# A mixture of experts as one large product: the first two stages of product 1 split a third time, their weight sums made in the first phase

## The chip, the cores and the metric

The kernel runs on one core of one Trainium2 chip. The metric is the device time of one execution in microseconds; for the kernel before it is the median of three runs, 1366.98 us (1366.88 to 1367.12). One more execution was taken by the hardware profiler: 1367.07 us, with a span from the first to the last instruction of 1365.1 us.

## The reference

16 x 512 = 8192 tokens with 512 values each, 8 experts, and a weight matrix of 512 x 2048 for each expert. Every token goes through all experts; the results are weighted by the softmax of its router logits and added up:

```python
probs = softmax(router_logits)                      # (16, 512, 8)
for e in range(8):
    output += probs[:, :, e:e+1] * np.matmul(x, expert_weights[e])
```

Since the weight of an expert can be multiplied into x first, this is one matrix product: 8192 rows, an inner dimension of 8 x 512 = 4096 (expert and hidden value), and 2048 columns.

## The kernel before

**Levels.** The kernel computes this product with the Strassen scheme (Winograd's form), in which a product of 2 x 2 blocks takes seven block products and some sums. On the outer level, the tokens come in pairs of blocks of 256 rows (`NHQ` = 32 blocks, 16 pairs, counted by `q`), the inner dimension in experts 0 to 3 and 4 to 7, the columns in two halves of 1024. The seven outer products are called 1 to 7; product 1 is the even block, experts 0 to 3, and the first column half. `product(r, q)` makes outer product `r` of pair `q`.

On the second level each outer product is split once more: 128 rows, two experts (eight chunks of 128, `K8`), 512 columns. Its seven **steps** go in the order 1, 5, 6, 2, 7, 3, 4 (`STEPS`, line 344). A step is eight TensorE matmuls of 128 x 128 by 128 x 512 into one PSUM bank (`Product.step`, line 543); `post` (line 551) then moves the bank on: a copy by ScalarE, or an addition by VectorE.

On the third level, which only some stages use, steps 1 and 5 of two products that run side by side are split again (`Split`, line 595, and `Third`, line 623). For each of the two steps there are seven **parts** of four matmuls of 128 x 128 by 128 x 256, named x1 to x7 for step 1 and q1 to q7 for step 5. The left side needs four sums of the two products' operands (tile `s`, `Third.make`), the right side four sums of blocks of the weight (tile `t`, `Split.make`), one set for each of the weights 1 and 5. Parts 6 and 7 are each followed by an addition on VectorE within PSUM (line 666), part 5 by two copies on ScalarE (lines 661 to 663).

**Left operands.** x times the probability, `z`, is made by VectorE from a transposed block `xT` and probabilities `pT` spread over all partitions (`times`, line 432). A stage's operands are `z` for the first two experts, the difference `d` of its token halves (`queue_s2`), `z` for the other two experts, and a combined one (`queue_i`).

**Weights.** Weight sums 5, 6, 7 and 4 of product 1 (tile `w`) are differences of the blocks in `b11` (`inner_sums`, line 169). Each takes one VectorE instruction of 4096 columns.

**The first phase** (lines 308 to 340) has no Strassen in it. It computes outer product 1 of pairs 0 and 1: four token tiles of 128 rows (`j`), two column halves (`n`), four experts (`e`), four chunks (`c`), 128 matmuls in all. Its left side `z0` is made by TensorE, which multiplies x by a diagonal matrix of probabilities (`early_z0`, line 246). In its second half (`n` = 1) TensorE also transposes blocks 4 to 7 for stage 0 (`early_xp1`, line 260; the casts out of PSUM are made by VectorE for `xT` and by ScalarE for `pT`), and VectorE makes weight sum 5. Its results go out through ScalarE copies and SyncE stores (lines 335 to 338). The softmax of all tokens is made meanwhile (`softmax_of_all`, line 284) and stored, so that later stages can load their probabilities.

**Stages.** After it come the stages, lists of one or two products that run step by step in turn (`run`, line 875). Stages 0 to 5 are product 1 of pairs 2 to 13, two pairs each. Stages 2 to 5 are split a third time (line 1219); the eight `t` sums for product 1 are queued in stage 1 (line 1221). When the next stage is split, the last two steps of a stage are held back (`held`, line 896) and run between the parts of the next: one behind parts 1 and 5, one behind parts 2 and 6 (`run_third`, line 856).

**What sets the order.** In the first phase a scheduler may move an instruction ahead on its engine, except on VectorE and ScalarE (`dve` and `act`, line 105), which keep the order of the program text. From line 342 on every engine keeps it. There the order of VectorE's work comes from a planner: work is put into `queue` with a cost, `slack` (line 375) takes from it while the planner's clock for VectorE is behind that for TensorE, and `need` (line 365) takes everything up to a task that must be there now. `at(stage, slot, ...)` hangs work on a place in a stage. Before stage 0, lines 1234 to 1242 fill the queue by hand: `z` of both products, weight sum 6, both `d`, the other `z`, weight sums 7 and 4.

**Buffers.** Weight tiles, `s` and `t` share one pool of 15 buffers (`wpool`, line 64); PSUM tiles come from a pool of 8 (line 95).

Of the kernel before, what the change touches and what calls it, by code (L numbers as in the profile page):

```python
# [31 lines left out]
def kernel(  # L32
# [7 lines left out]
    nc = tc.nc  # L40
    P = 128
    f16 = mybir.dt.float16
# [34 lines left out]
    def half():  # L77
        return h_tile([P, NB], f32)
# [43 lines left out]
    def sp(o, i):  # L122
        note(nc.sync.dma_start(out=o, in_=i))
# [7 lines left out]
    def mm(ps, z, w, start, stop):  # L131
        note(nc.tensor.matmul(ps, z, w, start=start, stop=stop, skip_group_check=True))  # L132
# [3 lines left out]
    def new_w():  # L136
        return wpool.tile([P, K8, NB], f16, name="w", tag="w")
# [122 lines left out]
    def early_xp1(j, d):  # L260
# [6 lines left out]
        mm(ps, ones, d.rearrange("p e t -> p (e t)"), True, True)  # L267
        evacuate(xp1[t][1][:, :, rows], ps.rearrange("p (e t) -> p e t", e=HE), 1)

    R = 4  # L270
    J = HQ // R
    p_dram = dram.tile([NHQ, 3 * HE, HQ], f16, name="p_dram")
# [32 lines left out]
                for c in (2 * g, 2 * g + 1) for j in (2 * h, 2 * h + 1)]  # L305
    ORDERS = [(c, j) for c in range(C) for j in range(4)], QUARTERS

    ds_ = [diag_e(0)]
    early_z0(0, ds_[0], (0, 1))
    for i in range(3):  # L310
# [4 lines left out]
    for e in (1, 2):  # L315
        ds_.append(diag_e(e + 1))
        early_z0(e, ds_[e])
    for n in range(2):
        ps = [bank() for _ in range(4)]
        for e in range(HE):  # L320
            if n == 0 and e == 1:
                early_z0(3, ds_[3])
                ph0.append(early_p(1))
                ds_ = [diag_j(j) for j in range(4, 8)]
                keep_p = softmax_of_all()
                w, sums = inner_sums(b11, new_w())
            for c, j in ORDERS[n == 0 and e == 0]:
                mm(ps[j], z0[j][:, e, c], b11[e // 2, n][:, e % 2 * C + c, :],
                   e + c == 0, e == HE - 1 and c == C - 1)
            if n == 1:  # L330
                for j in ((4, 5), (6, 7), (), ())[e]:
                    early_xp1(j, ds_[j - 4])
                if e == 1:
                    sums[5]()
        for j in range(4):
            o = half()
            act(nc.scalar.copy(o, ps[j]))
            sp(kept[j // 2][n].rearrange("(p j) m -> j p m", j=2)[j % 2], o)
        if n == 0:
            keep_p()  # L340

    ordered[0] = True
# [247 lines left out]


    THIRD = (1, 5)
    COLS = [ds(i * HQ, HQ) for i in range(2)]

    class Split:

# [8 lines left out]

        def make(self, p, i):
            if i == 0:
                self.t[p] = wpool.tile([P, 4, C, HQ], f16, name="t", tag="w")
            w, t = self.right.op(p), self.t[p]
            block = lambda k, n: w[:, ds(k * C, C), COLS[n]]  # L610
            x, y = ((block(0, 1), block(0, 0)), (block(1, 1), t[:, 0]), (block(1, 1), block(0, 1)),
                    (block(1, 0), t[:, 1]))[i]
            tt(t[:, i], x, y, SUB)

        def op(self, p, m):
            if m in (1, 2, 3):
                k, n = ((0, 0), (1, 0), (1, 1))[m - 1]
                return self.right.op(p)[:, ds(k * C, C), COLS[n]]
            i = {5: 0, 6: 1, 7: 2, 4: 3}[m]
            need(self.task[p, i])  # L620
            return self.t[p][:, i]

    class Third:
# [592 lines left out]
            post(p)  # L1216
    finish.step, finish.post = step_at_end, post_at_end

    for stage in (2, 3, 4, 5):
        third(stage, 1)  # L1220
    at(1, 2, splits[1].queue)
    for stage in (9, ):
        third(stage, 2)
    at(8, 2, splits[2].queue)
# [6 lines left out]
        third(stage, 3)  # L1231
    at(k3, 9, splits[3].queue)

    need_first = [right[1].task[p] for p in (6, 7, 4)]
    for p in (2, 3):
        lefts[1, p].queue_make(0)
    queue.append(need_first[0])
    for p in (2, 3):
        lefts[1, p].queue_s2()
    for p in (2, 3):  # L1240
        lefts[1, p].queue_make(1)
    queue.extend(need_first[1:])
    start_loads(1)
    store_loads(0)
    finish_loads(1)
# [30 lines left out]
```

## Time and profile before

| | before |
|---|---|
| median of 3 runs | 1366.98 us |
| profiled execution | 1367.07 us |
| its span | 1365.1 us |
| TensorE (PE) busy | 1359.9 us |
| VectorE (DVE) busy | 1126.5 us |
| ScalarE (ACT) busy | 195.7 us |
| matmuls | 6657 |
| VectorE instructions | 1367 |

In the profile PE is TensorE's matmuls, PEld its weight loads, DVE VectorE, ACT ScalarE, POOL GpSimd, SP SyncE, which only issues transfers. A row of the order of time shows the start in us from the first instruction, the duration in us, engine, line, operation, what is written and read with its shape, and xN for N like instructions in a row; behind it stands in brackets how long the engine had been idle and what released it. A row of the chain shows start, duration and what the end of the span hung on. A row of the waits shows the total, the number and the longest, in us. A row of busy time by stretches shows the stretch, its length, then the busy us of PE, PEld, DVE, ACT and POOL with the number of instructions, the granted clock, the busy share of the DMA engines and GB/s. All helpers issue through a few lines, so nearly all of VectorE's work has line 112 and TensorE's line 132; instructions are told apart by their tiles.

### The profile page before, as it was taken

The page shows a single profiled execution, that of the slowest core. Times are in us where ns is not written, and L with a number is a line of the kernel's source. Part 1 is how long each engine was busy: PE and PEld are TensorE (multiplying, and loading weights), DVE is VectorE, ACT ScalarE, POOL GpSimd, SP SyncE. Part 2 cuts the span into 40 slices and gives each one's busy share as a digit, 9 for nine tenths or more (in the row PEclk, how much of TensorE's full clock was granted, in tenths as well). Part 3 has the DMA queues.
Part 4 walks back from the last instruction along what each step waited for, and adds up shares of the span by engine and source line. Part 5 has one row for each costly group of instructions (what it writes and reads, how often), then busy time and mean ns, then how long its engine had stood idle before and what let it go on. Part 6 is the DMA issues. An engine that isn't in the chain of part 4 may idle for free.

```text
span 1365.1 us, 18194 instructions
## 1 busy us (share of the span) xinstructions
PE 1359.9 (100%) x6657; PEld 648.7 (48%) x6657; DVE 1126.5 (83%) x1367; ACT 195.7 (14%) x362; POOL 407.0 (30%) x644
## 2 busy tenths in 40 slices
PE   9999999999999999999999999999999999999998
PEld 4455544544444444444444444444444444456554
DVE  5975787989789788788887888888889797998873
ACT  3232311100011111111111100000000000123221
POOL 3123333331223342333322122242332422223232
PEclk9999999999999999999999999999999999999999
DMA  9999999999898999999999978989898979999896
GB/s 195 242 218 228 253 242 323 310 300 383 257 304 268 311 350 274 293 279 292 328 258 331 344 247 221 216 240 203 232 252 220 252 203 292 302 217 245 196 206 119
DMA packets 193385, 356.41 MB, mean 261 GB/s; under 512 B 53136, under 2 KB 87184, under 8 KB 188176
## 3 DMA queue, kind: packets, MB, share of 16 engines
q0 software_dynamic: 88048, 183.02, 55.3%
q1 hardware_dynamic: 99488, 132.25, 31.9%
q10 hardware_dynamic: 5760, 39.99, 7.6%
q8 instruction: 52, 0.85, 0.2%
q14 instruction: 37, 0.30, 0.1%
HBM read 214.47 MB, written 167.97 MB: 280 GB/s over the span
## 4 chain that ended last, share of the span: by engine, by line
PE 99%; DMA 0%; DVE 0%; issue 0%; ACT 0%; POOLq 0%
PE ps L132 99%; DMA w<-in_x_dram 0%; DVE z L238 0%; DVE h L112 0%; ACT h L1213 0%; POOLq L1260 0%
## 5 line engine op out<-in xcount | busy, mean ns | idle before, releaser
L132 PE MATMUL ps<-w,z 128*128 128x512 f16 x5240 | 1125.7, 375 | 0.0
L132 PEld LDWEIGHTS <-z 128*128 128x128 f16 x5328 | 521.2, 98 | 598.4
L126 POOL DMA_DIRECT2D out_dram<-h x380 | 249.3, 662 | 736.5 <-ACT h L582 352.6
L112 DVE TENSOR_TENSOR h<-ps,h 128x512 f32<-128x512 f32 x415 | 284.6, 687 | 184.7 <-PE ps L132 166.7
L112 DVE TENSOR_TENSOR z<-xT,pT 128x2048 f16<-128x2048 f16 x216 | 261.9, 1217 | 0.0
L132 PE MATMUL ps<-w,d 128*128 128x512 f16 x880 | 199.1, 379 | 0.0
L132 PEld LDWEIGHTS <-d 128*128 128x128 f16 x880 | 86.1, 98 | 101.5
L112 DVE TENSOR_TENSOR z<-z,d 128x2048 f16<-128x2048 f16 x110 | 131.7, 1217 | 0.0
L582 ACT COPY h<-ps 128x512 f32<-128x512 f32 x64 | 37.5, 585 | 524.5 <-PE ps L132 521.1
L112 DVE TENSOR_TENSOR w<-w 128x1024 f16<-128x1024 f16 (+2 forms) x88 | 100.0, 1146 | 1.8 <-PE ps L132 1.0
L571 ACT COPY h<-ps 128x512 f32<-128x512 f32 x90 | 52.7, 585 | 293.5 <-PE ps L132 264.1
L112 DVE TENSOR_TENSOR ps<-ps,h 128x512 f32<-128x512 f32 (+1 forms) x110 | 64.0, 585 | 26.0 <-PE ps L132 25.7
L112 DVE TENSOR_TENSOR d<-z 128x1024 f16<-128x1024 f16 x110 | 74.6, 687 | 5.1 <-PE ps L132 3.6
L568 ACT COPY h<-ps 128x512 f32<-128x512 f32 x90 | 51.8, 589 | 132.4 <-PE ps L132 129.6
L126 POOL DMA_DIRECT2D kept<-h x56 | 30.8, 549 | 110.9 <-ACT h L571 78.0
L126 POOL DMA_DIRECT2D wd<-w x78 | 44.2, 592 | 35.0 <-DVE w L112 27.5
L126 POOL DMA_DIRECT2D w<-in_expert_weights_dram x65 | 48.6, 778 | 19.5 <-issue 13.8
L112 DVE TENSOR_TENSOR u<-xT,pT 128x2048 f16<-128x2048 f16 x38 | 46.2, 1217 | 0.0
L112 DVE TENSOR_TENSOR h<-h 128x512 f32<-128x512 f32 (+2 forms) x69 | 45.1, 675 | 0.1
L112 DVE TENSOR_TENSOR z<-z,u 128x2048 f16<-128x2048 f16 x34 | 41.3, 1216 | 0.1
L112 DVE TENSOR_TENSOR z<-z 128x2048 f16<-128x2048 f16 x32 | 39.1, 1222 | 0.7
L564 ACT COPY ps<-ps 128x512 f32<-128x512 f32 x45 | 25.6, 570 | 94.4 <-PE ps L132 87.2
(61 smaller groups left out, 291.9 us busy)
## 6 DMA issues: line engine op xcount, KB each, us to landing
out_dram<-h POOLq DMA_DIRECT2D x380, 256.0 KB, 6.8
pT<-p_dram SPq DMA_DIRECT2D x125, 256.0 KB, 6.3
h<-kept SPq DMA_DIRECT2D x116, 256.0 KB, 6.7
w<-wd ACTq DMA_DIRECT2D x25, 1024.0 KB, 9.0
xT<-x SPq DMA_DIRECT2D x76, 256.0 KB, 6.8
w<-in_expert_weights_dram POOLq DMA_DIRECT2D x35, 512.0 KB, 10.9
wd<-w POOLq DMA_DIRECT2D x64, 256.0 KB, 6.6
h<-out_dram SPq DMA_DIRECT2D x60, 256.0 KB, 5.4
```

Of the source, the lines that this page charges most:

```text
L112: dve(nc.vector.tensor_tensor(out=o, in0=a, in1=b, op=op))
L126: note(nc.gpsimd.dma_start(out=o, in_=i, **how))
L132: note(nc.tensor.matmul(ps, z, w, start=start, stop=stop, skip_group_check=True))
L564: act(nc.scalar.copy(self.banks["b"], x))
L568: act(nc.scalar.copy(o[tn], q if p == 5 else x))
L571: act(nc.scalar.copy(o[TN[p]], b if p == 2 else x))
L582: act(nc.scalar.copy(o[tn], b))
```

## The change

The third level is used in stages 0 and 1 too, and with that several things move:

- The four `t` sums of weight 1 are made in the first phase: one ahead of the first products, three behind the last `z0`, ahead of the second softmax. The four of weight 5 are made behind weight sum 5, which itself comes one expert earlier. The `t` sums in stage 1 are gone.
- The last eight matmuls of the first phase (`n` = 1, `e` = 3, `c` = 2 and 3) are no longer made there. They are held as two lots of four and run in stage 0's places for held steps; the ScalarE copies and SyncE stores of these results follow the second lot.
- Stages 0 and 1 each get their left sums `s`, the parts, the additions and the copies. Before stage 0 the queue is filled with `z` of both products, the `s` sums, and weight sum 6, and emptied up to this; then come both `d`, the other `z`, and weight sum 7. Weight sum 4 is queued at the start of stage 0.
- In stage 0, the loads for stage 1 are issued ahead of the stores of the first phase's results, since these come later in the program.

In the order of the changed program VectorE has, from the casts of blocks 4 and 5: `xT` (2 casts), weight sum 5, four `t`, `xT` of blocks 6 and 7 (2 casts), two `z`, four `s`, weight sum 6, then stage 0's additions. TensorE has the transposes of blocks 4 to 7 five products into `n` = 1, `e` = 1, with some of that expert's products among them. From stage 2 on the order of every engine is as before, but for the eight `t`.

```diff
+    def third_weights(w, t, i):
+        block = lambda k, n: w[:, ds(k * C, C), COLS[n]]
+        x, y = ((block(0, 1), block(0, 0)), (block(1, 1), t[:, 0]), (block(1, 1), block(0, 1)),
+                (block(1, 0), t[:, 1]))[i]
+        tt(t[:, i], x, y, SUB)
...
+    early_t = {}
+
+    def early_thirds(p, some=range(4)):
+        if p not in early_t:
+            early_t[p] = new_t()
+        for i in some:
+            third_weights(w[p], early_t[p], i)
...
+    w, sums = inner_sums(b11, new_w())
+    early_thirds(1, (0,))
     for n in range(2):
         ps = [bank() for _ in range(4)]
         for e in range(HE):
             if n == 0 and e == 1:
                 early_z0(3, ds_[3])
+                early_thirds(1, (1, 2, 3))
                 ph0.append(early_p(1))
...
-                w, sums = inner_sums(b11, new_w())
             for c, j in ORDERS[n == 0 and e == 0]:
-                mm(ps[j], z0[j][:, e, c], b11[e // 2, n][:, e % 2 * C + c, :],
-                   e + c == 0, e == HE - 1 and c == C - 1)
+                if n == 0 or e < HE - 1 or c < 2:
+                    first_product(ps, n, e, c, j)
             if n == 1:
                 for j in ((4, 5), (6, 7), (), ())[e]:
                     early_xp1(j, ds_[j - 4])
-                if e == 1:
+                if e == 0:
                     sums[5]()
-        for j in range(4):
-            o = half()
-            act(nc.scalar.copy(o, ps[j]))
-            sp(kept[j // 2][n].rearrange("(p j) m -> j p m", j=2)[j % 2], o)
+                    early_thirds(5)
         if n == 0:
+            first_results(ps, n)
             keep_p()
...
-    for stage in (2, 3, 4, 5):
+    for stage in (0,1,2,3,4,5):
         third(stage, 1)
-    at(1, 2, splits[1].queue)
+    splits[1].t = early_t
...
+    def last_first(c):
+        for j in range(4):
+            first_product(ps, 1, HE - 1, c, j)
+        if c == C - 1:
+            first_results(ps, 1)
+
+    for c in (2, 3):
+        held.append(lambda c=c: last_first(c))
     need_first = [right[1].task[p] for p in (6, 7, 4)]
     for p in (2, 3):
         lefts[1, p].queue_make(0)
+    thirds[0].queue_sums()
     queue.append(need_first[0])
+    flush(need_first[0])
+    clock["dve"] = 0.0
     for p in (2, 3):
         lefts[1, p].queue_s2()
     for p in (2, 3):
         lefts[1, p].queue_make(1)
-    queue.extend(need_first[1:])
+    queue.append(need_first[1])
+    at(0, 0, lambda: queue.append(need_first[2]))
     start_loads(1)
```

`first_product` and `first_results` are the matmul and the copy with its store of before, made into functions; `new_t` makes a `t` tile. `Split.make` now calls `third_weights`, and `Split.op` asks for a queued task only where there is one.

More of the change, by code (lines that the diff above doesn't have):

```diff
@@ L268, in early_xp1, with new_t @@
         evacuate(xp1[t][1][:, :, rows], ps.rearrange("p (e t) -> p e t", e=HE), 1)
+    COLS = [ds(i * HQ, HQ) for i in range(2)]
+    def third_weights(w, t, i):
[3 more added lines that the diff above has]
+        tt(t[:, i], x, y, SUB)
+    def new_t():
+        return wpool.tile([P, 4, C, HQ], f16, name="t", tag="w")
+    early_t = {}
[4 more added lines that the diff above has]
+            third_weights(w[p], early_t[p], i)
     R = 4
@@ L306, with first_product, first_results @@
     ORDERS = [(c, j) for c in range(C) for j in range(4)], QUARTERS
+    def first_product(ps, n, e, c, j):
+        mm(ps[j], z0[j][:, e, c], b11[e // 2, n][:, e % 2 * C + c, :],
+           e + c == 0, e == HE - 1 and c == C - 1)
+    def first_results(ps, n):
+        for j in range(4):
+            o = half()
+            act(nc.scalar.copy(o, ps[j]))
+            sp(kept[j // 2][n].rearrange("(p j) m -> j p m", j=2)[j % 2], o)
     ds_ = [diag_e(0)]
@@ L592 @@
     THIRD = (1, 5)
-    COLS = [ds(i * HQ, HQ) for i in range(2)]
     class Split:
@@ L607, in make @@
             if i == 0:
[L608 to L613, printed above, removed]
+                self.t[p] = new_t()
+            third_weights(self.right.op(p), self.t[p], i)
         def op(self, p, m):
@@ L619, in op @@
             i = {5: 0, 6: 1, 7: 2, 4: 3}[m]
-            need(self.task[p, i])
+            need(self.task.get((p, i)))
             return self.t[p][:, i]
@@ L1232 @@
     at(k3, 9, splits[3].queue)
+    def last_first(c):
+        for j in range(4):
+            first_product(ps, 1, HE - 1, c, j)
[3 more added lines that the diff above has]
+        held.append(lambda c=c: last_first(c))
     need_first = [right[1].task[p] for p in (6, 7, 4)]
```

## The prediction

> **What bounds the kernel now.** I read the page first (busy shares and the chain that ended last), then the chain in order of time, then who waited on TensorE.
>
> ```profile
> span 1365.1 us, 18194 instructions
> PE 1359.9 (100%) x6657; PEld 648.7 (48%) x6657; DVE 1126.5 (83%) x1367; ACT 195.7 (14%) x362; POOL 407.0 (30%) x644
> ...
> PE 99%; DMA 0%; DVE 0%; issue 0%; ACT 0%; POOLq 0%
> ```
> ```profile
> 8.62 0.63 DVE h L112
> 9.25 0.05 issue
> 9.30 1352.25 PE ps L132 x6612
> ```
> ```profile
> PE every L94 <- DVE zero L91: 1.3, 1, 1.3
> PE ps L132 <- DVE h L112: 0.3, 1, 0.3
> ```
>
> From 9.30 us to the last product the chain is one unbroken piece of TensorE work, and TensorE's only waits on another engine lie before that. So time changes in two ways only: by the number and width of the products after 9.30 us, and by a stop of TensorE that isn't there now. What VectorE saves or spends counts only where TensorE comes to wait for it. The prices of products are read off the order of time on TensorE, first the start and stage 0, then a stage that is split a third time already:
>
> ```profile
> 1.30 4.45 PE L94 MATMUL every<-zero 128*128 128x512 f16 x10 [1.30 <-DVE zero L91]
> ...
> 7.50 1.50 PE L132 MATMUL ps<-h,w 128*128 128x128 f16 x24
> 9.30 1.07 PE L132 MATMUL ps<-h,w 128*128 128x128 f16 x16 [0.29 <-DVE h L112]
> ...
> 14.55 13.98 PE L132 MATMUL ps<-w,z 128*128 128x512 f16 x64
> 28.36 0.39 PE L132 MATMUL ps<-ident,w 128*128 128x128 f16 x4
> 28.58 0.38 PE L132 MATMUL ps<-h,ones 128*128 128x512 f16 x1
> ...
> 33.57 13.98 PE L132 MATMUL ps<-w,z 128*128 128x512 f16 x64
> ```
> ```profile
> 109.19 0.60 PE L132 MATMUL ps<-t,s 128*128 128x256 f16 x4
> 109.62 0.60 PE L132 MATMUL ps<-w,z 128*128 128x256 f16 x4
> 110.06 0.60 PE L132 MATMUL ps<-t,s 128*128 128x256 f16 x4
> 110.50 2.76 PE L132 MATMUL ps<-w,z 128*128 128x512 f16 x16
> ```
>
> A product 512 wide costs (28.36 - 14.55) / 64 = 0.2158 us from start to start. Groups of four 256 wide start 0.437 us apart, so one costs 0.109 us. The durations in the rows are longer, because products overlap.
>
> **What the split takes away.** In an unsplit stage, steps 1 and 5 of two products are 4 x 8 = 32 products 512 wide: 6.91 us. Split, they are 14 parts of 4, 56 products 256 wide: 6.11 us. Each stage saves 0.79 us, two stages **1.59 us**. Nothing else of TensorE's work changes in amount: the eight last products of the first phase move into stage 0, four behind the first parts and four behind the next, and the transposes of blocks 4 to 7 (28.36 us) fall among the first phase's second half.
>
> **The weight sums (t).** The eight sums leave stage 1, where VectorE has them at 76 to 81 us, and go into the first phase. Here are VectorE's rows of before, first its phase and stage 0, then the sums and the additions of a split stage:
>
> ```profile
> 14.08 1.29 DVE L238 CAST z<-ps 128x512 f16<-128x512 f32 x2 [1.84 <-PE ps L132]
> ...
> 22.86 2.20 DVE L112 TENSOR_TENSOR h<-h 128x512 f32<-128x512 f32 x4
> 28.78 1.29 DVE L238 CAST xT<-ps 128x512 f16<-128x512 f32 x2 [3.72 <-PE ps L132]
> 33.12 1.29 DVE L238 CAST xT<-ps 128x512 f16<-128x512 f32 x2 [3.04 <-PE ps L132]
> 34.44 2.29 DVE L112 TENSOR_TENSOR w<-w 128x4096 f16<-128x4096 f16 x1
> 36.65 2.35 DVE L112 TENSOR_TENSOR z<-xT,pT 128x2048 f16<-128x2048 f16 x2
> 38.92 2.28 DVE L112 TENSOR_TENSOR w<-w 128x4096 f16<-128x4096 f16 x1
> ...
> 59.76 0.69 DVE L112 TENSOR_TENSOR h<-ps,h 128x512 f32<-128x512 f32 x1
> ...
> 67.35 0.69 DVE L112 TENSOR_TENSOR s<-z 128x1024 f16<-128x1024 f16 x1
> ```
> ```profile
> 76.36 0.69 DVE L112 TENSOR_TENSOR t<-w 128x1024 f16<-128x1024 f16 x1
> ...
> 78.90 0.69 DVE L112 TENSOR_TENSOR t<-w 128x1024 f16<-128x1024 f16 x1
> ...
> 81.43 1.45 DVE L112 TENSOR_TENSOR h<-ps,h 128x512 f32<-128x512 f32 x2
> ...
> 90.42 0.87 DVE L112 TENSOR_TENSOR ps<-ps,h 128x256 f32<-128x256 f32 x2 [1.82 <-PE ps L132]
> ```
>
> Four t cost 81.43 - 78.90 = 2.53 us. The first four (of weight 1) are free: one fits into the 1.84 us of idle ahead of the last z0 casts at 14.08, the other three push the softmax chain from an end at 25.06 us to about 26.9, inside the 3.72 us of idle ahead of 28.78. If that cover were gone, the same 1.9 us would fall on the xT casts, and on the chain below. The second four (of weight 5) have no such cover: in the changed program they stand between sum 5 and the xT casts of blocks 6 and 7, and the first left operands (z) wait behind these.
>
> **Stage 0: who is late.** TensorE still begins its e=2 products at 33.57 us, but now only 24 of them come before stage 0: it gets there at 33.57 + 24 x 0.2158 = 38.75. Part x1 takes 0.44, and at **39.19** it wants part x5, whose left operand is the first sum of the two z (s). VectorE's path to it, with the rows' durations and their usual overlap of 0.08 us (none between an instruction and one that needs its result): the transposes of block 5 now start at 30.31 (28.36, and ahead of them seven first-phase products, block 4's four transposes, 0.22, and the product with ones, 0.22), their cast ends 30.31 + 0.39 + 0.03 + 0.69 = 31.42; sum 5 to 33.63; four t to the next start at 36.19; two xT casts to 37.40; two z, 37.40 to 39.75; s from 39.78 to 40.47. With 0.05 us to TensorE (VectorE ends at 9.25, TensorE resumes at 9.30) x5 starts at 40.52: a **stop of 1.33 us**. Before, stage 0 had no s and began at 33.57 + 32 x 0.2158 = 40.48, with its z ready at 37.9.
>
> Further on in stage 0 nothing more waits, but narrowly. Behind s stand its three others (to 42.52) and sum 6 (to 44.73), then the two additions of parts 6, to 45.08 and 45.52. Parts x7 and q7, which add into the columns that these read, come at 45.30 and 45.74, by the count below. I take nothing for it, and 0.3 us as the upper end.
>
> **Stage 1: the same once more.** From 40.52: x5, q1, q5 (1.31), four products (0.86), four parts (1.75), four products (0.86), six parts (2.62) end at 47.93; eight unsplit steps of 8 x 0.2158 = 1.73 end at 61.74; then stage 1's x1, and at **62.18** its x5. VectorE has by then, in the changed order, step 7's second result (its products end at 58.29, VectorE 58.49 to 59.18), z of one product (to 60.32), the first result of step 3 (60.24 to 60.93), z of the other (to 62.07), then the second result of step 3 (to 62.68), and only then s (62.60 to 63.29). x5 starts at 63.34: a **stop of 1.16 us**. What is queued behind here is s behind a result that TensorE itself finishes at 61.74; it is not a matter of lacking work time, so a quicker VectorE ahead of it would win little.
>
> The loads that stage 1 needs don't decide. SyncE's rows:
>
> ```profile
> 42.61 1.12 SPq L123 DMA_DIRECT2D pT<-p_dram  x2
> ...
> 44.80 6.22 SPq L407 DMA_TRANSPOSE xT<-w  x4
> ```
>
> In the changed order these stand ahead of the last stores of the first phase, no longer behind them, and even at the old times z at 59.1 has 8 us to spare. In later split stages VectorE has room:
>
> ```profile
> 84.00:107.50 23.50, 23.50 (x139) 13.37 (x137) 15.30 (x21) 6.94 (x14) 7.34 (x12) 1.00 0.98 234
> ```
>
> 15.3 us of 23.5 is VectorE's share in a split stage. So stage 2, which loses the t ahead of it, isn't late, and what is queued from there on stands as before. Stages 0 and 1 gain eight s (0.63 each) and eight additions (0.43): 8.5 us of VectorE work, none of which counts but for the two stops. ScalarE gains eight copies and is idle most of the time.
>
> **Sum.** -1.59 + 1.33 + 1.16 = +0.90 us on the profiled execution's 1367.07 us: 1367.97. The median of the runs is 0.09 lower, 1366.98, so I forecast **1367.9 us**. A stop's restart isn't in the trace at this length; I take 0.05 us, the one at 9.30, with 0 and 0.2 as ends. That and the narrow places give the forecast a range of its own of 1367.3 to 1368.6.
>
> **A rule that speaks against the saving.** The rows put a 256 wide product at 0.109 / 0.2158 = 0.51 of a 512 wide one; the split pays as long as that is under 32 / 56 = 0.57. The Trainium skill, page "TensorE: Matmul & The Clock Gate", section "Back-to-back issue gap", says that in streams of weight load and product the spacing is set by both, 81 ns at 128 columns and 131 ns at 512. An estimate midway from that page, some 98 ns at 256, would make the ratio 0.75 and the two stages 2.6 us longer where I count 1.59 shorter. The trace disagrees, with 0.2158 us at 512, and 0.109 at 256 in the very pattern that is added.
>
> **The rivals.**
> - *Both operands come in time, or one does.* VectorE is idle 17% of the span and 3.0 us just ahead of the row at 33.12. But the first sum stands behind everything counted above in program order, and moving 1.3 us out of that order needs an error in several rows. One stop alone gives 1366.7, none 1365.4; that is also the fastest that the change can be. Chance 0.10.
> - *More short stops*, at x7 and q7 of stage 0 (margins 0.2 us), with the same again in stage 1: 1368.6 to 1369.4. Chance 0.04.
> - *The clock falls when TensorE stops* (slower). The first ten products, 512 wide, took 4.45 / 10 = 0.44 us each, twice the later price; by the row at 7.50 the 128 wide ones run at 1.50 / 24 = 0.06. So the array was at half speed from 1.30 us to 7.50 at the latest, and such a stretch costs up to half its 6.2 us, 3.1 us. The stop of 0.29 us at 9.30 didn't bring it back; no stop of 1.3 us is in the trace. If the point lies between, one fall gives up to 1371.0 and two give up to 1374.1. For it: the same idle engine was slow at the start. Against: the granted clock is shown at 1.00 all along and these stops are a fraction of the stretch that it took to warm. Chance 0.07. The same page, section "What's actually happening", has half rate come back after an idle window of about 3.4 us; by that rule stops of 1.3 us leave the time at my forecast.
> - *Narrow products cost more than the trace shows*, by the rule above: the saving turns round and the stops remain, 1366.98 + 2.6 + 2.5 = 1372.1. Chance 0.01.
>
> **How the numbers follow.** The forecast has 0.78. The range, 1366.8 to 1369.2, takes in its own range and the nearer parts of the first two rivals; the clock, the case without a stop and the last rival stay outside, under 0.2 together. 0.2% is 2.73 us, about what a measurement of this kernel can tell from no change. Faster by that (under 1364.25) needs more than the whole saving: 0.01. Slower by that (over 1369.7) is the clock or the narrow products: 0.08. Within: 0.91.
>
> **What would show it.** Right: 48 more products in the changed profile; groups of four 256 wide 0.437 us apart in stages 0 and 1; TensorE waiting for VectorE's s twice, near 39 to 40.5 and 62 to 63.3 us, 1.1 to 1.4 us each; none later; 512 wide products at 0.216 us after each. Wrong: no wait for s (first rival), products at 0.4 us after a stop (clock), a wait at parts x7 and q7, or a wait for a load in stages 1 to 3.

## The result and the profile after

The kernel after takes **1374.4 us**, median of four runs (1372.3 to 1375.02); the kernel before took 1367.05 us beside it (1366.88 to 1367.13). The ratio is 1.005 with a 95% interval of 1.0038 to 1.0062: the change makes the kernel half a per cent slower. The profiled execution took 1375.02 us, 7.95 more than that of before. The page of after, in the same parts as before's (span, busy shares, the shares of the chain that ended last):

```profile
span 1373.1 us, 18308 instructions
PE 1361.0 (99%) x6705; PEld 652.8 (48%) x6705; DVE 1134.5 (83%) x1383; ACT 198.2 (14%) x370; POOL 407.0 (30%) x644
...
PE 88%; DMA 6%; issue 4%; POOL 1%; DVE 1%; SPq 0%; POOLq 0%; ACT 0%; DVEq 0%
```

The 48 products more that were counted are there (6705 against 6657), and so are the 16 VectorE instructions. But TensorE's share of the chain fell from 99% to 88%, and transfers hold 6% of it. The waits of TensorE, as total, number and longest, say where:

```profile
PE ps L132 <- DVE h L112: 3.6, 2, 3.3
PE ps L132 <- DVE s L112: 2.2, 2, 1.2
```

Two waits for `s` were forecast. The wait of 3.3 us for an `h` was not. TensorE's order of time at the first two, and then at the third:

```profile
10.59 3.63 PE L132 MATMUL ps<-w,z 128*128 128x512 f16 x16 [0.95 <-DMA w<-in_expert_weights_dram]
...
34.32 5.78 PE L132 MATMUL ps<-w,z 128*128 128x512 f16 x28
41.34 0.61 PE L132 MATMUL ps<-t,s 128*128 128x256 f16 x4 [1.23 <-DVE s L112]
41.78 0.60 PE L132 MATMUL ps<-w,z 128*128 128x256 f16 x4
...
52.20 10.96 PE L132 MATMUL ps<-w,z 128*128 128x512 f16 x52
64.18 0.61 PE L132 MATMUL ps<-t,s 128*128 128x256 f16 x4 [1.02 <-DVE s L112]
```
```profile
158.59 0.60 PE L132 MATMUL ps<-t,s 128*128 128x256 f16 x4
162.49 5.28 PE L132 MATMUL ps<-w,z 128*128 128x512 f16 x16 [3.31 <-DVE h L112]
167.56 1.38 PE L132 MATMUL ps<-t,s 128*128 128x256 f16 x8
```

The first stop: 24 products 512 wide and four 256 wide from 34.32 end their turn at 34.32 + 24 x 0.2158 + 4 x 0.109 = 39.94; part x5 starts at 41.34, so 1.40 us are lost (1.33 forecast). The second: 52.20 + 48 x 0.2158 + 4 x 0.109 = 63.0, resumed at 64.18, 1.18 us (1.16 forecast). The third is at the start of stage 5. There the 16 products after the stop, eight 512 wide and eight 256 wide, take 5.07 us up to the next start; at 0.2158 and 0.109 each they would take 2.60. Busy time by stretches (length, then PE, PEld, DVE, ACT, POOL with counts, then the granted clock):

```profile
158.90:161.40 2.50, 0.28 (x3) 0.10 (x2) 2.50 (x4) 0.80 (x3) 0.00 (x0) 1.00 1.15 400
161.40:162.50 1.10, 0.01 (x1) 0.01 (x1) 1.10 (x3) 0.00 (x0) 0.00 (x0) 0.51 1.17 200
162.50:168.20 5.70, 5.70 (x19) 2.82 (x19) 5.22 (x6) 0.58 (x1) 4.11 (x8) 0.50 1.06 376
168.20:176.00 7.80, 7.80 (x52) 4.99 (x51) 6.81 (x9) 3.31 (x6) 1.17 (x3) 1.00 1.05 272
```

The granted clock is halved from 161.4 to 168.2 us: TensorE resumes at 162.49 and does 5.7 us at half rate, which loses half of it, about 2.9 us. With the wait itself, 3.3, the place costs some 6.2 us. The account of the profiled executions:

| part | us |
|---|---|
| start: the products of `e` = 2 begin at 34.32 instead of 33.57 | +0.75 |
| two stages split | -1.59 |
| stop at stage 0 | +1.40 |
| stop at stage 1 | +1.18 |
| stop at stage 5, waiting and half clock | +6.2 |
| sum (measured 7.95) | +7.94 |

The 0.75 us is a later arrival of the first loads, such as the 0.95 in the row at 10.59; the profiles of experiments 1, 2 and 12, which have the same first phase, begin those products at 33.37, 33.79 and 33.89.

**Why `h` is late at 159 us.** VectorE's order of time before it:

```profile
140.81 1.23 DVE L112 TENSOR_TENSOR z<-xT,pT 128x2048 f16<-128x2048 f16 x1 [1.00 <-DMA xT<-xs]
...
154.29 1.23 DVE L112 TENSOR_TENSOR z<-xT,pT 128x2048 f16<-128x2048 f16 x1 [11.57 <-issue]
...
161.75 1.88 DVE L112 TENSOR_TENSOR h<-ps,h 128x512 f32<-128x512 f32 x3
```

VectorE, 83% busy, stands still for 11.57 us in front of a `z` of stage 5. Behind it in VectorE's order come four `s`, two `d` and two more `z`, and only then, at 161.75, the `h` that TensorE waits for. The row names no releaser ("issue"); what the `z` reads tells it. The two transposes (by DMA) that write its x block `xT` were issued at 140.8 and 142.2. This is how long the two transfers took in after, and then those of before for the same `z`:

```profile
L436 SPq DMA_TRANSPOSE xT<-xs x2: 1300/1452/1604, 140.8 to 142.2; - x2
...
DMA to landing us min/median/max: 8.9/10.5/12.1
```
```profile
L407 SPq DMA_TRANSPOSE xT<-xs x2: 1214/1260/1307, 127.1 to 128.4; - x2
...
DMA to landing us min/median/max: 2.4/2.7/3.0
```

In after the second lands at 142.15 + 12.05 = 154.2, just before `z` starts; in before both had landed by 131.4. So the question is why these transposes are issued 14 us later. The chain of after answers that from 96 us on:

```profile
96.09 7.78 DMA xs<-in_x_dram
103.89 1.19 SPq L436
105.13 11.43 DMA xT<-xs
116.65 1.19 SPq L436
117.88 2.50 DMA xT<-xs
...
120.97 6.64 DMA xs<-in_x_dram
127.63 1.26 SPq L436
128.94 11.80 DMA xT<-xs
140.81 8.94 DMA xT<-xs
```

It is a loop through buffers. A stage's x blocks are loaded into `xs`, transposed in two pairs (the second pair is written only when the first has landed), and the next stage's load waits until the second pair has landed. From one load to the next, 96.09 to 120.97, the chain has no gap but 0.5 us of issuing: the loop takes 24.9 us, more than the 23.4 us of a stage, so as long as it takes that, a delay is not made up. How it got late shows in SyncE's rows (from the first transposes' issue to the end of the fourth's), before and then after:

```profile
73.28 10.35 SPq L407 DMA_TRANSPOSE xT<-xs  x4
```
```profile
75.97 18.29 SPq L436 DMA_TRANSPOSE xT<-xs  x4
...
127.63 16.12 SPq L436 DMA_TRANSPOSE xT<-xs  x4
```

The first four start 2.7 us later, but take 18.3 us instead of 10.4. GpSimd's queue, before and after, shows what stands beside them:

```profile
66.26 1.48 POOL L126 DMA_DIRECT2D xs<-in_x_dram  x2
67.70 1.53 POOL L126 DMA_DIRECT2D w<-in_expert_weights_dram  x2
```
```profile
64.35 0.73 POOL L126 DMA_DIRECT2D xs<-in_x_dram  x1
73.63 0.74 POOL L126 DMA_DIRECT2D xs<-in_x_dram  x1 [8.55 <-DVE z L112]
...
74.93 1.50 POOL L126 DMA_DIRECT2D w<-in_expert_weights_dram  x2
```

The second x load of stage 3 waits for a `z` of stage 1, because it needs a buffer that this `z` reads (`xs`, `xT` and `pT` share one pool of 9 buffers, line 67). VectorE's rows of the last `z` of stage 1, before and then after:

```profile
58.63 1.22 DVE L112 TENSOR_TENSOR z<-xT,pT 128x2048 f16<-128x2048 f16 x1
...
60.96 1.22 DVE L112 TENSOR_TENSOR z<-xT,pT 128x2048 f16<-128x2048 f16 x1
```
```profile
72.12 2.35 DVE L112 TENSOR_TENSOR z<-xT,pT 128x2048 f16<-128x2048 f16 x2
```

They come 12 to 13 us later, since stage 1, now split, has its `s`, `d` and additions first. Behind the load in GpSimd's queue stand two loads of the weights of experts 4 to 7 (`b21`) which convert to half precision, 512 KB each. They move from 67.7 to 74.9, onto the first transposes. That gives **theory A**, a late start of the loop, with **theory B** as its rival, the converting loads beside the transposes; the experiments separate these two, the two early stops and the clock.

### The profile page after: what moved, and what is told of

It reads as the page before. It is cut to its first block, busy times and chain, and to the rows that moved or that the text cites. A ratio compares the mean times of both kernels' runs of the same rounds, so it can differ in the third digit from the quotient of the medians.

```text
span 1373.1 us, 18308 instructions
## 1 busy us (share of the span) xinstructions
PE 1361.0 (99%) x6705; PEld 652.8 (48%) x6705; DVE 1134.5 (83%) x1383; ACT 198.2 (14%) x370; POOL 407.0 (30%) x644
## 4 chain that ended last, share of the span: by engine, by line
PE 88%; DMA 6%; issue 4%; POOL 1%; DVE 1%; SPq 0%; POOLq 0%; ACT 0%; DVEq 0%
PE ps L132 88%; DMA xT<-xs 3%; DMA w<-in_x_dram 1%; DMA xs<-in_x_dram 1%; DMA kept<-h 1%; POOL w L126 1%; POOL kept L126 0%; SPq L436 0%; DVE z L112 0%; DVE s L112 0%; DVE d L112 0%; DVE h L112 0%; POOL xs L126 0%; ACT h L1237 0%; POOLq L126 0%
## 5 line engine op out<-in xcount | busy, mean ns | idle before, releaser
L132 PE MATMUL ps<-w,z 128*128 128x512 f16 (+1 forms) x5208 | 1119.3, 376 | 4.4 <-DVE h L112 3.3
L112 DVE TENSOR_TENSOR ps<-ps,h 128x512 f32<-128x512 f32 (+1 forms) x118 | 67.2, 574 | 28.0 <-PE ps L132 27.3
L132 PEld LDWEIGHTS <-s 128*128 128x128 f16 x416 | 40.7, 98 | 10.5 <-DVE s L112 2.8
L132 PE MATMUL ps<-t,s 128*128 128x256 f16 x312 | 42.9, 274 | 2.2 <-DVE s L112 2.2
```

The lines of the kernel that those rows point to most:

```text
L112: dve(nc.vector.tensor_tensor(out=o, in0=a, in1=b, op=op))
```

## The experiments

Times are medians, with the range of the runs; the kernel before stood between 1367.03 and 1367.28 beside them. In the experiments a pair is the two transposes of one x block of 256 x 512, and its time is counted from the first issue to the last landing.

**1. `z` of stage 1 early.** The second two `z` of stage 1 are made right behind its `s`, ahead of `d`.

```diff
+            if stage == 1:
+                for left in two:
+                    left.queue_make(1)
             left.queue_s2()
...
+    at(1, 1, lambda: flush(stages[1][1].left.task[1]))
```

> The changed kernel, but stage 1's z for the second two experts is made right behind its s sums, in VectorE's idle time at 66 to 68 us, no longer behind the additions at 72 to 74.5. Theory A (the buffers of x and probabilities that stage 1 holds come free too late, so that the loads for stages 3 to 5 start some 10 us later and their chain of load, transpose, transpose never wins it back): stage 3's loads start at 68 us or before, its second pair of transposes lands before 90 us (95.5 in the changed kernel), the stop of TensorE near 159 us is gone and with it the half clock; time 1368.0 to 1368.7 us. Theory B (transposes are slow because they run beside the casting loads of the weights, whatever their start): landing times of the transposes stay at 11 to 15 us, the stop stays; 1372 to 1375 us.

1368.15 us (1367.47 to 1369.56), ratio 1.0007 (0.9998 to 1.0016). The stop at stage 5 is gone; the two early ones stay, 1.40 and 1.18. The x load issues at 66.66 instead of 73.63. So the late stop hangs on the place of this `z`; this is theory A's value, but B is not refuted, since the converting loads move to 67.96 too.

**2. Only stage 0 split, and 3. only stage 1 split.**

```diff
-    for stage in (0,1,2,3,4,5):
+    for stage in (0, 2, 3, 4, 5):
```

> The changed kernel with stage 0 split a third time and stage 1 not. Theory A: stage 1 makes all its z before 63 us as in the kernel before, so its buffers are free early, and there is no stop near 159 us; what is left is one saving of 0.79 and the first stop of 1.4: 1367.6 us (0.7 more if the first weights land late at the start, as they did in the changed kernel's profile). If instead the work put into the first phase or the late stores of its results delay the loads, the late stop stays: 1371 us or more.

1367.9 us (1367.44 to 1368.44), ratio 1.0003 (0.9994 to 1.0012): one stop behind the first phase, 1.39 us, and no late one, as theory A expected, though the last `z` of stage 1 ends at 66.6 and not before 63. The late stores of the first phase are in this kernel too, so they alone don't make the late stop.

```diff
-    for stage in (0,1,2,3,4,5):
+    for stage in (1, 2, 3, 4, 5):
...
-                if n == 0 or e < HE - 1 or c < 2:
-                    first_product(ps, n, e, c, j)
+                first_product(ps, n, e, c, j)
...
+        first_results(ps, n)
...
-            first_results(ps, n)
...
-    for c in (2, 3):
-        held.append(lambda c=c: last_first(c))
...
-    thirds[0].queue_sums()
...
-    flush(need_first[0])
-    clock["dve"] = 0.0
...
-    queue.append(need_first[1])
-    at(0, 0, lambda: queue.append(need_first[2]))
+    queue.extend(need_first[1:])
```

> The changed kernel with stage 1 split a third time and stage 0 not; all products of the first phase are made in the first phase again. Theory A: the late stop near 159 us is there, with the fall of the clock, since it comes from stage 1's order; no stop at stage 0, and that at stage 1 is smaller or gone, since VectorE has fewer sums behind it: 1366.3 us plus 3 to 6.5 us, so 1369 to 1373. Theory B: depends on where the transposes fall beside the casts; as the start of the loads is hardly different from the changed kernel's, the same. Without any late stop: 1366.3 us, and both theories would be short of something in stage 0.

1366.27 us (1366.06 to 1367.23), ratio 0.9993 (0.9984 to 1.0002): **missed**. There is no stop at 40, 62 or 159 us; x5 of stage 1 starts at 61.62, as soon as x1 is done (50.83 + 48 x 0.2158 + 4 x 0.109), and the last pair of transposes lands at 131.5. Stage 1's split alone makes its first `s` at 56.9 (63.4 in after), and the first of the two last `z`, which ends at 59.9 in before, at 64.2; the second x load goes out at 64.46, not late. It takes both splits: each alone moves that `z` by 4 to 5 us (64.7 in experiment 2), both by 13 (73.3 in after).

**4. The converting loads later.** In the stages where they stand at place 2, they go to place 9; nothing else moves.

```diff
-        at(i + 1, 2, lambda kn=kn: cast21(kn))
+        at(i + 1, 9, lambda kn=kn: cast21(kn))
```

> The changed kernel with the casting loads of the weights of stages 1 to 4 (b21) begun at place 9 of the stage, no longer place 2, some 10 us later. Theory B: the transposes of stages 3 and 4, now free of them, land within 4 to 9 us each, and the late stop is gone: 1368 to 1368.7 us. Theory A: stage 3's loads still start at 73 us, 10 us later than in the kernel before; the stop near 159 us stays, perhaps smaller: 1370 to 1375 us.

1368.35 us (1367.91 to 1370.9), ratio 1.0009 (1.0001 to 1.0018). No late stop, though the loop still begins late (its first transposes at 75.74). The first pairs take 8.3, 5.8 and 5.2 us instead of 15.7, 12.7 and 13.1. So a late start alone isn't enough, and theory B holds its half.

**5. Sum 5 early**, behind the softmax and so ahead of the casts of blocks 4 and 5:

```diff
+                sums[5]()
...
-                    sums[5]()
```

> The changed kernel with weight sum 5 (2.2 us of VectorE) made right behind the softmax, in VectorE's idle time at 27 to 30 us, no longer between the xT casts. If the stop at stage 0 is the time that VectorE's row of work runs over, as the prediction worked it out, it is gone (1.39 us), and the one at stage 1 stays at 1.2 us, since its s waits behind a result that TensorE itself finishes. For the late stop: the loads of stages 3 to 5 are bound to the release of stage 1's buffers and to their own chain, and these move by no more than 1.4 us. If the chain of loads sets the end of the late stop, TensorE gets there 1.4 us earlier and waits as much longer: 1372 to 1375 us. If the late stop hangs on where in the stage the transposes fall, it can vanish: 1366.8 us.

1372.37 us (1370.57 to 1373.56), ratio 1.0037 (1.0024 to 1.0049). The stop at stage 0 is gone, the one at stage 1 is 1.18 as in after, and the late stop stays (a wait of 3.79 us), with a small stop of 1.0 us ahead of it at 142. The order of VectorE that the prediction blamed for the first stop is its cause.

**6. All three stops taken away:** experiments 1 and 5, and `s` of stage 1 made at place 9 of stage 0.

```diff
+    at(0, 9, lambda: flush(thirds[1].task[0]))
+    at(1, 1, lambda: flush(stages[1][1].left.task[1]))
```

> The changed kernel with three orders of VectorE's work changed: weight sum 5 right behind the softmax; stage 1's first two z and the first s ahead of the second result of step 7 and both of step 3; and stage 1's other two z right behind its s. If the stops at stages 0 and 1 and the late release of buffers are all that the change lost, none of the three stops is left and the time is that of the products alone, 1.59 us under the kernel before: 1365.4 to 1365.7 us. If the split has a further cost that these stops hid, 1366.5 us or more.

1365.95 us (1365.12 to 1367.66), ratio 0.9993 (0.9984 to 1.0002). No stop at 40, 62 or 159 us. It is the fastest median of all kernels here, 1.1 us under before on the same chip, but the interval reaches past 1, and it lies between the two expected cases (up to 1365.7, or from 1366.5). Its profiled execution, 1366.27, is 0.80 under before's 1367.07. The saving of 1.59 fits that: the products of `e` = 2 begin 0.18 us later (33.75 instead of 33.57), and small stops between 1169 and 1214 us cost 0.62; -1.59 + 0.18 + 0.62 = -0.79.

**7. Stops alone.** The kernel before, with a stop of growing length at place 8 of stages 17 to 30. The two small products of each stop write into a bank that the kernel uses, so that some sums of those stages are disturbed.

```diff
+    def stop(n):
+        b = bank()
+        mm(b[:, 0:P], ident, ident, True, True)
+        act(nc.scalar.copy(pause, b[:, 0:P]))
+        for _ in range(n):
+            act(nc.scalar.copy(pause, pause))
+        mm(b[:, 0:P], pause, ident, True, True)
+    for i in range(14):
+        at(17 + i, 8, lambda n=3 + i: stop(n))
```

> The kernel before with 14 stops of TensorE put in, one in each of stages 17 to 30, by 4 to 17 dependent ScalarE copies of 128 x 128 between two small products; estimate from the 0.37 us of a 256 wide copy: some 0.26 us each, so stops of about 1.1 to 4.6 us, 40 us in all. Theory 1 (the clock falls by how much of a fixed stretch of some 3.4 us TensorE stood idle, and needs not be idle all through it): stops up to about 1.7 us never halve it, stops from 2.3 to 3.4 us do in some cases, and all above do; each fall lasts two such stretches, 6.8 us, and costs 3 us: 5 to 10 falls, 1420 to 1440 us. Theory 2 (a whole stretch must be idle): only stops over 3.4 us can, and not all of these: 1 to 4 falls, 1408 to 1420 us. If stops of 1.1 to 1.7 us halve it too, the two stops in stages 0 and 1 were only lucky.

One run, 1445.18 us. The sizes missed: a copy took 0.33 us, so the stops are 1.8 to 6.1 us of idle time, longer than planned, and so is the time. TensorE's rows of the fifth and sixth stop, and then the stretches behind them:

```profile
559.11 0.23 PE L132 MATMUL ps<-ident,pause 128*128 128x128 f16 x1 [3.09 <-ACT pause L1250]
587.00 0.23 PE L132 MATMUL ps<-ident,pause 128*128 128x128 f16 x1 [3.42 <-ACT pause L1250]
```
```profile
559.50:563.00 3.50, 3.50 (x18) 1.57 (x16) 0.80 (x2) 0.00 (x0) 1.22 (x2) 1.00 1.02 370
...
587.00:588.20 1.20, 1.20 (x7) 0.61 (x8) 0.00 (x0) 0.00 (x0) 0.00 (x0) 1.00 1.01 376
588.30:591.70 3.40, 3.40 (x10) 1.21 (x8) 0.69 (x1) 0.00 (x0) 0.54 (x1) 0.50 0.95 384
591.80:594.00 2.20, 2.20 (x12) 1.02 (x11) 0.69 (x1) 0.00 (x0) 0.54 (x1) 1.00 0.67 267
```

After 3.09 us of idle time the clock stays at 1.00, after 3.42 it is at 0.50 for a while. So it is with all fourteen: none of the five stops up to 3.09 us halves the clock, all nine from 3.42 on do. That is theory 1's count (5 to 10 falls), not theory 2's (1 to 4). But the length alone doesn't decide: in after 3.31 us of idle time was enough. What the falls have in common is in the last section; by it the stops of 1.0 to 1.2 us in after are on the safe side.

**8. The last converting load later.** Only the one of the fourth stage moves to place 9, so that fewer stand beside the last pair.

```diff
-        at(i + 1, 2, lambda kn=kn: cast21(kn))
+        at(i + 1, 9 if i == 3 else 2, lambda kn=kn: cast21(kn))
```

> The changed kernel with only the last of the four casting loads of b21 moved from place 2 to place 9 of stage 4, so that at 139 to 142 us two loads are issued, not four. If the late stop needs that burst (the last pair of transposes, issued at 140.8, lands at 154.2 among it, and at 5 us beside nothing), the pair lands by about 150 and the stop is gone or short of 1 us: 1368.0 to 1369 us. If the late start of the chain alone makes the stop, it stays: 1372 to 1375 us.

1374.7 us (1372.23 to 1375.03), ratio 1.0052 (1.0038 to 1.0066): the time of the second case, but not its single stop. The last pair still takes 11.1 us and lands at 152.4, with two converting loads beside it; several small stops between 142 and 227 us, of 0.2 to 1.6 us each, take the place of the large one. What each of them hangs on wasn't followed. The profile of this run shows no half clock. Thinning the crowd at 140 us doesn't mend it; by then the loop is late.

**9. A late start in the kernel before.** The x loads of stage 3, and SyncE's loads of the probabilities, wait for a result of stage 1; the x loads start at 74.8 us, with the converting loads ahead of them.

```diff
+    late[1] = 6
...
+    def wait_here():
+        o = products[1, 4].o[0, 1]
+        pool(gate[0], o[:, 0:8])
+        sp(gate[1], o[:, 0:8])
+    at(1, 5, wait_here)
```

> The kernel before, with nothing split anew, but the loads of x and probabilities for stage 3 held back on GpSimd's and SyncE's queues behind the store of a few columns of a result of stage 1 that is there at 73.5 us. They start there at 74 us (67 before; 73.6 is when the changed kernel issues its second one). If a late start of stage 3's loads is enough, whatever TensorE and VectorE do, the pairs of transposes land later from stage to stage (95, 119, 140 to 155 us, where the kernel before has 87, 108, 131), VectorE waits for x near 140 us and TensorE stops near 155 us, with a fall of the clock: 1370 to 1373 us. If the chain wins the delay back, or the late stop needs something else of the change, 1367.0 us.

1366.93 us (1366.54 to 1368.78), ratio 1.0 (0.9991 to 1.0009). GpSimd's and SyncE's rows:

```profile
66.14 1.54 POOL L126 DMA_DIRECT2D w<-in_expert_weights_dram  x2
74.24 0.57 POOL L126 DMA_DIRECT2D gate<-h  x1 [6.56 <-ACT h L568]
74.80 1.43 POOL L126 DMA_DIRECT2D xs<-in_x_dram  x2
```
```profile
81.38 5.16 SPq L407 DMA_TRANSPOSE xT<-xs  x4
```

The transposes start 5.4 us later than in after, and nothing is lost: with the converting loads gone by, all four are issued within 5.2 us instead of 18.3, the second pair lands at 88.9, and the loop is back at its usual times one stage on. "A late start alone is enough" is refuted.

**10. The first three converting loads later.**

```diff
-        at(i + 1, 2, lambda kn=kn: cast21(kn))
+        at(i + 1, 2 if i == 3 else 9, lambda kn=kn: cast21(kn))
```

> The changed kernel with the first three of the four casting loads of b21 at place 9 of stages 1 to 3, the fourth left at place 2 of stage 4: the counterpart of the kernel that moved the fourth alone. If the chain falls behind because its transposes run beside these three loads, stage by stage, the first transposes of each pair of blocks take 5 to 9 us, no longer 13 to 16, x for stage 5 lands by 145 us in spite of the burst, and there is no late stop or one under 1 us: 1368.0 to 1369 us. If the start of the chain alone counts, or the burst at 139 us, it stays: 1372 to 1375 us.

1369.84 us (1368.35 to 1375.48), ratio 1.0027 (1.0016 to 1.0039): between the two cases. The first pairs are fast (7.7, 5.6 and 5.0 us), the last pair lands at 134.7, and the profiled execution, 1369.29, lost 0.89 us ahead of 164.75. But three of eleven executions took 1374 and more, and one 1372.5; what happened in these has no profile and stays open.

**11. No early stops.** Experiment 5 and `s` of stage 1 at place 9 of stage 0, the `z` where the change has it.

```diff
+    at(0, 9, lambda: flush(thirds[1].task[0]))
```

> The changed kernel without its stops at stages 0 and 1 (weight sum 5 right behind the softmax; stage 1's first two z and the first s ahead of the second result of step 7), but stage 1's other two z left behind the additions, as in the changed kernel. If the late stop comes from the late release of buffers by these z, it stays, and TensorE only gets to it sooner: no stop at 40 and 62 us, the stop near 157 us with a half clock, 1370.5 to 1373 us. If the two early stops had thrown the chain of loads out of step, it is gone: 1365.4 to 1366 us, the same as the kernel with all three orders changed.

1371.37 us (1369.53 to 1372.7), ratio 1.0028 (1.0018 to 1.0037). Both early stops are gone, the late one stays: a wait of 3.37 us, with 3.4 us of half clock. The early stops neither make the late one nor add to it.

**12. The first two converting loads ahead of the x loads.** In stage 1, the two converting loads go ahead of the two x loads on GpSimd's queue. VectorE's and SyncE's orders stay as the change has them.

```diff
-        at(i + 1, 2, lambda kn=kn: cast21(kn))
+        at(i + 1, 0 if i == 0 else 2, lambda kn=kn: cast21(kn))
```

> The changed kernel with one thing moved: stage 1's casting loads of b21 stand ahead of the two loads of x for stage 3 on GpSimd's queue (place 0), no longer behind them (place 2). VectorE's and SyncE's orders are the same. In the changed kernel the second load of x waits for a buffer until 73.6 us, and the casts behind it start at 74.9 and run beside stage 3's transposes (76.0 to 91.7). If it takes both, late loads and casts beside the first transposes, then the casts start at 64 us and land by 77, the first transposes take 5 to 9 us, both pairs have landed by 91, stages 4 and 5 are in step as in the kernel before, and there is no late stop: 1368.0 to 1368.6 us. If the late buffers alone decide, the chain is as late as in the changed kernel and the stop near 159 us stays: 1372 to 1375 us.

1368.28 us (1367.9 to 1370.19), ratio 1.0008 (0.9999 to 1.0017). GpSimd's and SyncE's rows:

```profile
63.91 1.53 POOL L126 DMA_DIRECT2D w<-in_expert_weights_dram  x2
...
73.19 0.72 POOL L126 DMA_DIRECT2D xs<-in_x_dram  x1 [7.05 <-DVE z L112]
```
```profile
75.64 10.52 SPq L436 DMA_TRANSPOSE xT<-xs  x4
```

The x load waits for `z` just as long (to 73.19), and the first transposes start as late (75.64). But they take 10.5 us, the loop recovers, and only the two forecast stops remain, 1.39 and 1.18. This is the narrowest cut: a late x load alone doesn't make the late stop, it takes the converting loads held behind it in the same queue. Whether those would do it alone, with the x loads on time, isn't shown: no run has them so.

The transposes of all these kernels in one table: issue of the first pair of stage 3 and its time to landing, the same time for stages 4 and 5, and the landing of the last pair of stage 5.

| kernel | issued at | stage 3 | stage 4 | stage 5 | last pair lands | late stop |
|---|---|---|---|---|---|---|
| before | 73.3 | 7.8 | 9.1 | 9.4 | 131.4 | no |
| 9 (before, late x loads) | 81.4 | 5.5 | 9.3 | 9.7 | 131.4 | no |
| after | 76.0 | 15.7 | 12.7 | 13.1 | 154.2 | yes |
| 11 (no early stops) | 72.7 | 16.1 | 12.8 | 13.1 | 151.7 | yes |
| 5 (sum 5 early) | 74.3 | 15.8 | 13.0 | 13.7 | 154.1 | yes |
| 8 (last one later) | 75.3 | 15.9 | 12.9 | 13.4 | 152.4 | small ones |
| 1 (`z` early) | 70.0 | 12.3 | 10.4 | 9.4 | 133.2 | no |
| 12 (first ones ahead) | 75.6 | 7.7 | 9.6 | 9.4 | 133.8 | no |
| 4 (all later) | 75.7 | 8.3 | 5.8 | 5.2 | 140.4 | no |
| 10 (three later) | 75.6 | 7.7 | 5.6 | 5.0 | 134.7 | small one |

## Why the prediction was wrong, step by step

- **What bounds the kernel: right.** Only stops of TensorE, the amount of its products and, for 2.9 us, their half rate moved the time; the half rate stood among the rivals. The account above closes with these.
- **The split, -1.59: right in its prices.** The groups of four start 0.44 us apart in stage 0, there are 48 products more, and in experiment 3, with one stage split, stage 1's products with `d` begin at 70.75 instead of 71.56, 0.81 us earlier (0.79 expected).
- **The stop at stage 0, 1.33 us: right.** 1.40 measured; it goes with sum 5 (experiment 5).
- **The stop at stage 1, 1.16 us: right.** 1.18 measured; it goes when `s` is made earlier (experiment 11). That it is "not a matter of lacking work time" holds for its place behind a result in after's order, but the stop needs a split stage 0 too: without it `s` is made before that result (experiment 3).
- **The narrow places x7 and q7, nothing: right.** TensorE has no wait there.
- **"What is queued from there on stands as before": the step that failed.** From stage 2 on the order stands; the times do not. The prediction looked at the loads that stage 1 needs and at VectorE's work in later stages, 15.3 of 23.5 us, and found room. It did not ask when stage 1's own second `z` would be made, which buffer that frees, and which load in GpSimd's queue waits for it, with what behind it. The `z` comes some 13 us later (its end at 73.3 instead of 59.9), the load 7.4 us (66.26 to 73.63), the converting loads 7.2 (67.70 to 74.93), and stage 5 pays 6.2 us for it 85 us on. Its list of signs had "a wait for a load in stages 1 to 3" as a sign against it, but gave it no price; TensorE's stop came in stage 5.
- **The clock: the rival's mechanism came, at another stop.** The point looked for between 0.29 and 1.3 us isn't there: the two stops that it was priced for left the clock alone. It fell at the stop that was not forecast, and brought 2.9 of its 6.2 us. That the rival's upper end, 1374.1, comes near the 1374.4 measured is luck.
- **The range** had the case of a large stop later on nowhere. The sum without that stop is 1375.02 - 6.2 = 1368.8, of which 0.75 is the start: in the range.

What stays open: why the first pairs beside the converting loads take 12.7 to 15.7 us in after and 7.8 to 9.4 in before. The traces show so much: in before each of these pairs lands 0.8 to 1.2 us behind the second converting load beside it, in after 2.2 to 4.0 behind, and in after that load itself takes 13.0 to 13.9 us instead of 10.9 to 11.8. So both are slow together. The phase between the two and the stores may matter; it wasn't tried. The small stops of 0.3 to 0.6 us in all at 1169 to 1214 us in experiments 1, 3, 6 and 11 are open too.

## What to carry to other kernels

When work is added to an engine that has room, follow not only who waits for its results but which buffers its reads hold, and which load waits for these; then count everything queued behind that load as moved too. A loop of load, transpose and release that takes as long as a stage (here 24.9 us against 23.4) makes up no delay, and the bill may come several stages later; with the converting loads out of its way the loop was back in step a stage on (experiment 9). Room on an engine says nothing about room in the transfers.

## What the runs showed of the hardware

**The clock falls without a whole window of idleness.** In after TensorE's last product ends at 159.2, and the granted clock is halved from 161.4, 2.2 us later. In experiment 7 the stop of 3.42 us ends at 587.0, and the clock is still 1.00 up to 588.2 and falls only then, for 3.4 us (the rows stand with the experiment).

All falls in experiment 7 start on one raster of 3.41 us and last one or two steps of it. The Trainium skill, page "TensorE: Matmul & The Clock Gate", section "What's actually happening", tells of a free-running window of 3413 ns and of half rate after at least one idle window. The raster agrees. But in the step before the fall at 588.3, from 584.9, TensorE was idle for 2.1 of 3.41 us only, so a window need not be idle as a whole; the measurement decides.

How much of a step must be idle can be read off the same raster. These are two steps of experiment 7 (behind the length stands PE's busy time), the first with 1.98 us of idle time, the second with 2.14:

```profile
673.60:677.01 3.41, 1.43 (x8) 0.51 (x6) 2.83 (x3) 2.14 (x7) 1.60 (x3) 1.00 0.85 292
...
704.32:707.73 3.41, 1.27 (x7) 0.46 (x5) 2.46 (x4) 2.11 (x8) 2.36 (x5) 1.00 0.97 329
```

After the first the clock stayed at 1.00, after the second it fell to 0.50, at 707.73. Of all steps at full rate between the start-up and the last product, in all traces here, none with up to 1.98 us idle was followed by a fall, and each of the twelve with 2.14 to 3.41 was (nine in experiment 7; 2.23 in after, 2.20 in experiment 11, 2.99 in experiment 5). So in these traces the idle time within one step decides, and the bound lies between 1.98 and 2.14 of 3.41 us. The stops of 3.09 and less in experiment 7 each left at most 1.82 in one step; a stop of 2.1 to 3.3 us that lies in one step as a whole wasn't tried.

**DMA transposes are slow beside converting loads.** The two transposes of a block of 256 x 512 take 5.0 to 8.3 us from the first issue to the last landing where the converting loads are out of the way (the first pairs of experiments 4 and 10, and those of stage 3 in experiments 9 and 12). Beside them they take 7.8 to 9.4 us in before, and 12.7 to 16.1 in after and experiments 5, 8 and 11.
